# Sixty-four transposes of a two-layer hybrid decoder trunk: TensorE with an identity, or VectorE in 32 x 32 squares

## The chip, the core and the metric

The kernel runs on one core of a Trainium2 chip. The metric is the device time of one launch in microseconds (us), lower is better. A core has TensorE (PE in the profile; PEld is its weight load), VectorE (DVE), ScalarE (ACT), GpSimd (POOL) and the queue engine SyncE (SP). SBUF is the memory that all engines work in, PSUM the one that TensorE writes to; both have 128 partitions.

## The reference

A trunk of two layers works on x, 256 positions by 2048 numbers, in fp32. Each layer normalises x and multiplies it by `w_in` (2048 x 7700). Four parallel groups of 4 heads, 512 columns each, use the result:

```python
h = rms_norm(x, norm_g)
p = split_columns(jnp.einsum("bsd,de->bse", h, w_in))
fox = from_heads(forgetting_attention(q, k, v, log_f)) * silu(p["fox_g"])   # softmax attention with a forget bias
diff = rms_norm(differential_attention(...), diff_norm_g) * silu(p["diff_g"])
moba = from_heads(moba_attention(...)) * silu(p["moba_g"])                  # 256 positions: one block, causal attention
gla = from_heads(rms_norm(gla_chunked(...), gla_norm_g)) * silu(p["gla_g"]) # gated linear attention
mixed = jnp.concatenate([fox, diff, moba, gla], axis=-1)
x = x + jnp.einsum("bse,ed->bsd", mixed, w_out)
```

After the second layer a last `rms_norm` follows.

## The kernel before

**The large products.** `w_in` and `w_out` come from memory in steps of 512 KB (two or four blocks of 128 rows of the weights, "k-tiles"). ScalarE rounds each step to a high part `hi`, VectorE subtracts it for the low part `lo` (`parts_of`, `hi_of`, `lo_of`), and TensorE forms three products, high by high, low by high and high by low. The activations are kept with their 2048 numbers on the partitions, transposed, and split in the same way: `hTp` (the normalised x, high and low) for `w_in`, `mTh` and `mTl` (the four groups' results) for `w_out`. There are four buffers for the raw weights and four for each part. In the main loop (line 1335) step i + 3 is prepared (`prepare`), then step i is multiplied (`multiply`), then the small work gets a turn (`tick`).

**The small work.** All that lies between the large products is written as generators, one per group and purpose, in a list `tasks`. `tick` lets each of them go on to its next `yield`, so that their instructions fall between two steps of the large products. `Costed` adds up an assumed time for each VectorE and ScalarE instruction, and `give_time` grants as much as TensorE's matmuls are assumed to take; a tick stops while more is used than granted. So the program order on every engine is fixed when the kernel is built. Tiles are handed out by `Slots`: eight of 128 x 1024 in SBUF (`s4`, named `four`), six of 128 x 512 (`s2`, `two`), two of 128 x 1024 in PSUM (`side`). A generator that finds no free slot yields until there is one.

**The three places.** Everything that must stand the other way round is transposed by TensorE, with an identity, 128 x 128 at a time, into a `side` tile (`transpose`, line 286, matmul at L288 in the profile; all other matmuls of this part are at L284):

- `make_hT` (line 422) prepares x for the second layer, in four chunks of 512 columns, each as soon as the output projection of the first layer has added its chunk to `xs`: `turn_x` makes 8 transposes, `split_x` makes high and low parts from PSUM.
- `finish_rows` (line 506) normalises and gates the output rows of the differential and of the linear attention (`mixed`) and transposes them, 8 transposes per group and layer.
- `transposed_p` (line 729) transposes the softmax probabilities: `p0` (queries 0 to 127, keys 0 to 127) and `p1` (queries 128 to 255, all 256 keys), 8 and 4 transposes, with a copy by ScalarE to `pta` and one by VectorE to `ptb`. All three softmax attentions call it; the forgetting and the block attention through `attend_columns` (line 760), which then forms the output with v:

```python
matmul(o[:, h], vn[:, 0, h * P:(h + 1) * P], pta[:, h], True, False)
matmul(o[:, h, P:], vn[:, 1, h * P:(h + 1) * P], ptb[:, h], False, True)
```

The order of the layer's blocks is: linear attention, forgetting attention, differential attention, block attention, then four chunks of the output projection, whose k-tiles begin with the linear attention's and end with the block attention's. In the first layer x comes transposed from memory, so `make_hT` runs for the second layer alone.

Of the kernel before, what the change touches and what calls it, by code (L numbers as in the profile page):

```python
# [21 lines left out]
P = 128  # L22
SEQ = 256
# [3 lines left out]
H = 4  # L27
# [190 lines left out]
def hybrid_trunk(  # L218
# [18 lines left out]
    v_ = Costed(nc.vector, 0.06, 1.05e-3)  # L237
# [12 lines left out]
    s4 = Slots(wk, "four", T4)  # L250
    s2 = Slots(wk, "two", T2)
    s8 = Slots(wk, "eight", 1)
    sgs = Slots(wk, "gate", 2)
    side = Slots(sd, "side", 2)

    def take_side():
        return (yield from side.take([P, 1024]))
# [24 lines left out]
    def matmul(out, lhsT, rhs, start, stop, tiles=1):  # L282
        left["pe"] += int(np.prod(rhs.shape[1:])) * (4 if lhsT.dtype == F32 else 1) / 2400.0 / tiles
        t_.matmul(out, lhsT, rhs, start=start, stop=stop)  # L284

    def transpose(out, src):
        left["pe"] += 0.109
        t_.transpose(out, src, ident)  # L288


    ct = cp.tile([P, KEPT], F32, name="ct")
    ngt = cp.tile([P, DEPTH, KT], F32, name="ngt")
    xs = big.tile([P, 2, D], F32, name="xs")
# [86 lines left out]
    def before_pow(ss, n, inv):  # L380
        t = sm.tile([P, 8], F32, name="pw")
        v_.tensor_scalar(t[:, :n], ss, inv, EPS, op0=OP.mult, op1=OP.add)
        return t[:, :n]

    def power(dst, t, n):
        g_.tensor_tensor(dst, t, halfpow[:, :n], op=OP.pow)  # L386

    def hi_of(hi, src, scale=1.0):
        a_.activation(hi, src, AF.Copy, scale=scale)

    def lo_of(lo, src, hi):
        v_.tensor_sub(lo, src, hi.bitcast(F32))
# [7 lines left out]
    def turn_x(ps, chunk):  # L400
        for k in range(4):
            for m in range(2):
                kt = chunk * 4 + k
                transpose(ps[:, k * 256 + m * P:k * 256 + (m + 1) * P], xs[:, m, kt * P:(kt + 1) * P])

    def split_x(ps, l, chunk):

        cols = [(chunk * 4 + k, ps[:, k * 256:(k + 1) * 256]) for k in range(4)]
        for kt, src in cols:
            hi_of(hT[0][:, kt], src, ngt[:, l, kt:kt + 1])  # L410
        for kt, src in cols:
            v_.scalar_tensor_tensor(hT[1][:, kt], src, ngt[:, l, kt:kt + 1], hT[0][:, kt].bitcast(F32),
                                    op0=OP.mult, op1=OP.subtract)
        side.put(ps)
        ready.add(("h", l, chunk))

    def squares(l, chunk, parts):
        for m in range(2):
            square_sum(parts, m, slice(chunk * 512, chunk * 512 + 512), chunk)
        ready.add(("sq", l, chunk))  # L420

    def make_hT(l, chunk, parts):
        if chunk < 3:
            yield
        ps = yield from take_side()
        turn_x(ps, chunk)
        yield
        split_x(ps, l, chunk)
        yield
        squares(l, chunk, parts)  # L430

# [49 lines left out]
    def transposes(nat):  # L481

        ps = yield from take_side()
        for h in range(H):
            for m in range(2):
                transpose(ps[:, h * 256 + m * P:h * 256 + (m + 1) * P], nat[:, m, h * P:(h + 1) * P])
        return ps

    def split_group(l, gi, src, release):
        kts = slice(gi * 4, gi * 4 + 4)  # L490
        hi_of(mT[0][:, kts], src)
        yield
        lo_of(mT[1][:, kts], src, mT[0][:, kts])
        release()
        ready.add(("m", l, gi))
# [10 lines left out]
    def finish_rows(l, gi, o, ops, scale, sg):  # L506

        sq = yield from s4.take([P, 2, H, HD])
        a_.activation(sq, o, AF.Square)
        yield  # L510
        ss = sm.tile([P, 2, H], F32, name="ssh")
        v_.tensor_reduce(ss, sq, axis=AX.X, op=OP.add)
        s4.put(sq)
        if scale is not None:
            v_.tensor_mul(ss, ss, scale)
            v_.tensor_mul(ss, ss, scale)
        t = before_pow(ss.rearrange("p m h -> p (m h)"), 8, 1.0 / HD)
        rs = sm.tile([P, 2, H], F32, name="rsh")
        power(rs.rearrange("p m h -> p (m h)"), t, 8)
        yield  # L520
        yield
        if scale is not None:
            v_.tensor_mul(rs, rs, scale)
        mixed = yield from gated_rows(l, gi, o, rs, sg)
        side.put(ops)
        sgs.put(sg)
        yield
        ps = yield from transposes(mixed)
        s4.put(mixed)
        yield  # L530
        yield from split_group(l, gi, ps.rearrange("p (h t) -> p h t", h=H), lambda: side.put(ps))
# [194 lines left out]
        side.put(ps)  # L726
        return p

    def transposed_p(p0, p1, pool0=s2, slot0=None):
        ta = yield from take_side()  # L730
        for h in range(H):
            transpose(ta[:, h * 256:h * 256 + P], p0[:, h])
            transpose(ta[:, h * 256 + P:(h + 1) * 256], p1[:, h, 0])
        pool0.put(p0 if slot0 is None else slot0)
        yield
        pta = yield from s4.take([P, H, 2, P])
        a_.activation(pta.rearrange("p h m q -> p (h m q)"), ta, AF.Copy)
        side.put(ta)
        tb = yield from take_side()
        for h in range(H):  # L740
            transpose(tb[:, h * P:(h + 1) * P], p1[:, h, 1])
        s4.put(p1)
        yield
        ptb = yield from s2.take([P, H, P])
        v_.tensor_copy(ptb.rearrange("p h q -> p (h q)"), tb[:, :512])
        side.put(tb)
        yield
        return pta, ptb

    def normalised(p0, p1, su):  # L750
        rs = sm.tile([P, 2, H], F32, name="rs")
        v_.reciprocal(rs, su)
        v_.tensor_mul(p0, p0, rs[:, 0, :, None].to_broadcast([P, H, P]))
        yield
        pv = p1.rearrange("p h j s -> p h (j s)")
        v_.tensor_mul(pv, pv, rs[:, 1, :, None].to_broadcast([P, H, SEQ]))
        yield
        return (yield from transposed_p(p0, p1))

    def attend_columns(l, gi, name, qT, kT, forget=None):  # L760

        su = sm.tile([P, 2, H], F32, name="su")
        p0 = yield from softmax_part(0, qT, kT, slice(0, P), HD ** -0.5, su, forget)
        p1 = yield from softmax_part(1, qT, kT, slice(0, P), HD ** -0.5, su, forget)
        s4.put(qT, kT)
        if forget is not None:
            forget.release()
        yield
        pta, ptb = yield from normalised(p0, p1, su)
        yield from until((name + "_v", l))  # L770
        yield from until((name + "_g", l))
        yield
        vn, sgT = env[name + "_v", l], env[name + "_g", l]
        ops = yield from take_side()
        o = ops.rearrange("p (h t) -> p h t", h=H)
        for h in range(H):
            matmul(o[:, h], vn[:, 0, h * P:(h + 1) * P], pta[:, h], True, False)
            matmul(o[:, h, P:], vn[:, 1, h * P:(h + 1) * P], ptb[:, h], False, True)
        s4.put(pta, vn)
        s2.put(ptb)  # L780
        yield
        mixed = yield from s4.take([P, H, SEQ])
        v_.tensor_mul(mixed, o, sgT)
        side.put(ops)
        sgs.put(sgT)
        yield
        yield from split_group(l, gi, mixed, lambda: s4.put(mixed))
# [20 lines left out]
    class Forget:  # L808
# [16 lines left out]
        def release(self):  # L825
            s4.put(*self.fg)
            s2.put(*self.f1)
# [135 lines left out]
    def diff(l):  # L963
# [4 lines left out]
        scale = 64 ** -0.5  # L968
        su = [sm.tile([P, 2, H], F32, name="su") for _ in range(2)]
# [13 lines left out]
        ps = yield from take_side()  # L983
# [9 lines left out]
        p0 = yield from s4.take([P, 2, H, P])  # L993
        for i in range(2):
            for h in range(H):
                c = i * H + h
# [20 lines left out]
        p1 = []  # L1017
# [12 lines left out]
        c = sm.tile([P, 2, H], F32, name="nr")  # L1030
        v_.tensor_mul(c, rs[1], su[0])
        v_.tensor_scalar(c, c, lam[:, l:l + 1], -1.0, op0=OP.mult, op1=OP.mult)
        for m, a, b in ((0, p0[:, 0], p0[:, 1]), (1, p1[0], p1[1])):
            for h in range(H):
                v_.scalar_tensor_tensor(a[:, h], b[:, h], c[:, m, h:h + 1], a[:, h], op0=OP.mult, op1=OP.add)
            yield
        s4.put(p1[1])
        pta, ptb = yield from transposed_p(p0[:, 0], p1[0], s4, p0)
        yield from until(("diff_v", l))
        yield  # L1040
        vn = env["diff_v", l]
        ops = yield from take_side()
        o = ops.rearrange("p (m h d) -> p m h d", m=2, h=H)
        for h in range(H):
            matmul(o[:, 0, h], pta[:, h, 0], vn[:, 0, h * P:(h + 1) * P], True, True)
        for h in range(H):
            matmul(o[:, 1, h], pta[:, h, 1], vn[:, 0, h * P:(h + 1) * P], True, False)
            matmul(o[:, 1, h], ptb[:, h], vn[:, 1, h * P:(h + 1) * P], False, True)
        s4.put(pta, vn)
        s2.put(ptb)  # L1050
        yield
        yield from until(("diff_g", l))
        yield from finish_rows(l, 1, o, ops, rs[0], env["diff_g", l])
# [86 lines left out]
    for z in _BLOCKS:  # L1140
        if z["half"] != 1:
            l, f = next(dones)
# [5 lines left out]
    for z in _steps():  # L1148
        b = blocks[z["block"]]
# [185 lines left out]
    for i, s in enumerate(plan):  # L1335
# [3 lines left out]
        if i in X_AT:  # L1339
            c = slice(X_AT.index(i) * 512, X_AT.index(i) * 512 + 512)  # L1340
# [11 lines left out]
    b = plan[-1]["block"]  # L1352
# [29 lines left out]
```

## Time and profile before

| | |
|---|---|
| device time, median of 3 runs | 948.75 us (948.12 to 948.85) |
| profiled execution, its own time | 950.85 us |
| its span, first to last instruction | 949.1 us |
| instructions | 13841 |
| TensorE matmuls, busy | 5430, 938.4 us |
| VectorE, busy | 836 instructions, 613.7 us |
| ScalarE, busy | 653 instructions, 482.5 us |
| granted TensorE clock, mean of the core | 0.996 |

Busy times of the engines overlap; their sum is no time. The ends of matmuls are modelled, so a busy TensorE isn't one at its peak. An fp32 matmul leaves two records. Nearly all VectorE and ScalarE instructions have one line, L188, that of the helper which books their costs; they are told apart by their tiles.

### The profile page before, as it was taken

How to read it: one execution, taken by the hardware profiler on the slowest of the kernel's cores; microseconds unless marked ns; L12 is line 12 of the kernel's file. 1: busy time of each engine (PE TensorE's matmuls, PEld its weight loads, DVE VectorE, ACT ScalarE, POOL GpSimd, SP SyncE). 2: the span in 40 equal slices, each digit the busy share in tenths (PEclk: the TensorE clock that was granted, in tenths of full speed). 3: DMA queues.
4: the chain of work that ended last, by engine and by line, in shares of the span. 5: the costliest groups of instructions: out<-in, count | busy, mean ns of one | idle time of the engine just before them, and what ended most of it. 6: DMA issues, size and time to landing. Idle time of an engine off the chain costs nothing.

```text
span 949.1 us, 13841 instructions
## 1 busy us (share of the span) xinstructions
PE 938.4 (99%) x5430; PEld 823.0 (87%) x5430; DVE 613.7 (65%) x836; ACT 482.5 (51%) x653; POOL 68.4 (7%) x45
## 2 busy tenths in 40 slices
PE   9999999999999999999999999999999999999996
PEld 7889899888888888888898899898888898888886
DVE  7566785657756786455556667656675759755563
ACT  7575534454474446445446544446446644564451
POOL 0010201001110210000000102100011002100000
PEclk9999999999999999999999999999999999999998
DMA  8766555455656465566655544554555645754552
GB/s 298 225 186 214 185 185 173 140 172 179 198 170 178 147 206 176 159 193 182 189 172 175 165 149 156 168 176 156 167 189 177 198 152 178 238 179 160 195 178 89
DMA packets 49076, 170.19 MB, mean 179 GB/s; under 512 B 5969, under 2 KB 6513, under 8 KB 49010
## 3 DMA queue, kind: packets, MB, share of 16 engines
q1 hardware_dynamic: 46592, 165.24, 54.8%
q10 hardware_dynamic: 1778, 1.97, 0.9%
q0 software_dynamic: 640, 2.10, 0.9%
q8 instruction: 42, 0.69, 0.3%
q14 instruction: 24, 0.20, 0.1%
HBM read 167.19 MB, written 2.10 MB: 178 GB/s over the span
## 4 chain that ended last, share of the span: by engine, by line
PE 95%; DMA 2%; DVE 1%; issue 1%; ACT 0%; SPq 0%; POOLq 0%; POOL 0%; DVEq 0%; ACTq 0%
PE mm L284 86%; PE side L284 8%; PE side L288 2%; DMA raw<-in_weights 1%; DMA four<-in_xt 1%; DVE lo L188 0%; ACT hi L188 0%; DVE xs L188 0%; ACT hTp L188 0%; DVE four L188 0%; SPq L1159 0%; POOLq L1378 0%; POOL rf L386 0%; ACT two L188 0%; SPq L1172 0%
## 5 line engine op out<-in xcount | busy, mean ns | idle before, releaser
L188 DVE TENSOR_TENSOR lo<-raw,hi 128x1024 fp32r<-128x1024 f32 (+3 forms) x301 | 380.0, 1269 | 288.1 <-ACT hi L188 287.7
L188 ACT ACTIVATE hi<-raw 128x1024 fp32r<-128x1024 f32 (+3 forms) x301 | 318.4, 1060 | 406.5 <-PE mm L284 373.2
L284 PE MATMUL mm<-hTp,hi 128*128 128x512 f32 x1120 | 273.1, 392 | 0.0
L284 PEld LDWEIGHTS mm<-hTp,hi 128*128 128x128 f32 x1120 | 204.3, 188 | 39.4 <-issue 0.3
L284 PE MATMUL mm<-hi,hTp 128*128 128x512 f32 (+2 forms) x1024 | 196.6, 339 | 0.3 <-ACT hi L188 0.3
L284 PEld LDWEIGHTS mm<-hi,hTp 128*128 128x128 f32 x1024 | 159.8, 188 | 22.0 <-ACT hi L188 0.8
L284 PE MATMUL mm<-hTp,lo 128*128 128x256 f32 x1120 | 150.0, 284 | 0.0
L284 PEld LDWEIGHTS mm<-hTp,lo 128*128 128x128 f32 x1120 | 144.8, 191 | 5.9
L284 PE MATMUL mm<-lo,hTp 128*128 128x512 f32 (+2 forms) x512 | 104.9, 336 | 0.1
L284 PEld LDWEIGHTS mm<-lo,hTp 128*128 128x128 f32 x512 | 81.3, 188 | 10.4 <-DVE lo L188 0.3
L284 PE MATMUL mm<-hi,mTh 128*128 128x512 f32 (+1 forms) x256 | 65.1, 378 | 0.0
L284 PE MATMUL mm<-hi,mTl 128*128 128x512 f32 (+1 forms) x256 | 64.4, 376 | 0.0
L284 PE MATMUL mm<-lo,mTh 128*128 128x512 f32 (+1 forms) x256 | 64.4, 376 | 0.0
L284 PEld LDWEIGHTS mm<-hi,mTl 128*128 128x128 f32 x256 | 46.2, 188 | 8.8
L284 PEld LDWEIGHTS mm<-lo,mTh 128*128 128x128 f32 x256 | 46.2, 188 | 8.7
L284 PEld LDWEIGHTS mm<-hi,mTh 128*128 128x128 f32 x256 | 45.7, 188 | 8.3
L284 PE MATMUL side<-four,four 128*128 128x128 f32 (+2 forms) x288 | 38.0, 288 | 0.0
L920 POOL TENSOR_TENSOR four<-four,two 128x1024 f32<-128x1024 f32 x8 | 20.9, 2607 | 222.4 <-DVE four L188 222.4
L188 ACT ACT_TABLE_LOAD x27 | 34.6, 1283 | 2.0 <-DVE an L188 1.5
L284 PEld LDWEIGHTS side<-four,four 128*128 128x128 f32 (+1 forms) x288 | 31.5, 190 | 2.6 <-issue 1.4
L188 DVE TENSOR_TENSOR both<-mm,both 128x512 f32<-128x512 f32 x35 | 23.9, 684 | 0.0
L386 POOL TENSOR_TENSOR rsh<-pw,halfpow 128x8 f32<-128x8 f32 x4 | 10.4, 2590 | 152.1 <-DVE pw L188 152.1
(159 smaller groups left out, 620.8 us busy)
## 6 DMA issues: line engine op xcount, KB each, us to landing
raw<-in_weights SPq DMA_DIRECT2D x272, 512.0 KB, 3.8
raw<-in_weights SPq DMA_DIRECT2D x16, 516.0 KB, 3.7
raw<-in_weights SPq DMA_DIRECT2D x15, 528.0 KB, 4.6
xs<-in_x SPq DMA_DIRECT2D x4, 512.0 KB, 4.5
four<-in_xt SPq DMA_DIRECT2D x3, 512.0 KB, 7.5
out<-xs SPq DMA_DIRECT2D x6, 256.0 KB, 3.1
two<-in_const POOLq DMA_DIRECT2D x4, 256.0 KB, 3.4
two<-in_final_norm_g POOLq DMA_DIRECT2D x4, 256.0 KB, 5.7
```

Source lines behind the costliest of these rows:

```text
L188: return f(*args, **kw)
L284: t_.matmul(out, lhsT, rhs, start=start, stop=stop)
L288: t_.transpose(out, src, ident)
L386: g_.tensor_tensor(dst, t, halfpow[:, :n], op=OP.pow)
L920: g_.tensor_mul(sw, sw, over(f[:, 1], H))
```

## The change

A new helper `turned` transposes a 128 x 128 block, or several side by side, on VectorE: for each of the 4 x 4 squares of 32 partitions by 32 columns one `transpose` instruction, which takes that square of all blocks of the tile together. It yields after each four. It is used for chunks 0 to 2 of x, for the gated rows of the linear attention (`scale is None`) and for the probabilities of the forgetting attention. The fourth chunk of x, the differential attention and the probabilities of the other attentions stay on TensorE. The result lies in SBUF (`s4`, `s2`) and not in PSUM, and is split from there. Since the forgetting attention's probabilities now come in three tiles, `attend_columns` multiplies by three tiles of 128 columns, for the block attention too.

```diff
+    def turned(dst, src):
+        for j in range(4):
+            for i in range(4):
+                a, b = slice(32 * i, 32 * i + 32), slice(32 * j, 32 * j + 32)
+                v_.us += 0.14
+                v_.transpose(dst[(b,) + (slice(None),) * (len(dst.shape) - 2) + (a,)],
+                             src[(a,) + (slice(None),) * (len(src.shape) - 2) + (b,)])
+            yield
...
     def make_hT(l, chunk, parts):
         if chunk < 3:
             yield
-        ps = yield from take_side()
-        turn_x(ps, chunk)
-        yield
-        split_x(ps, l, chunk)
+        if chunk < 3:
+            t = yield from s4.take([P, 4, SEQ])
+            rows = xs[:, :, chunk * 512:chunk * 512 + 512].rearrange("p m (k c) -> p m k c", k=4)
+            yield from turned(t.rearrange("p k (m t) -> p m k t", m=2), rows)
+            split_x(t.rearrange("p k t -> p (k t)"), l, chunk)
+            s4.put(t)
+        else:
+            ps = yield from take_side()
+            turn_x(ps, chunk)
+            yield
+            split_x(ps, l, chunk)
+            side.put(ps)
...
+        if scale is None:
+            t = yield from s4.take([P, H, SEQ])
+            yield from turned(t.rearrange("p h (m t) -> p m h t", m=2), mixed.rearrange("p m (h d) -> p m h d", h=H))
+            s4.put(mixed)
+            yield from split_group(l, gi, t, lambda: s4.put(t))
+            return
         ps = yield from transposes(mixed)
...
-    def transposed_p(p0, p1, pool0=s2, slot0=None):
+    def transposed_p(p0, p1, by_rows, pool0=s2, slot0=None):
+        if by_rows:
+            pt0 = yield from s2.take([P, H, P])
+            yield from turned(pt0, p0)
+            pool0.put(p0 if slot0 is None else slot0)
+            pt1 = yield from s4.take([P, H, 2, P])
+            yield from turned(pt1, p1)
+            s4.put(p1)
+            return [pt0, pt1[:, :, 0], pt1[:, :, 1]], lambda: (s2.put(pt0), s4.put(pt1))
...
-        pta, ptb = yield from normalised(p0, p1, su)
+        pt, release = yield from normalised(p0, p1, su, name == "fox")
...
         for h in range(H):
-            matmul(o[:, h], vn[:, 0, h * P:(h + 1) * P], pta[:, h], True, False)
-            matmul(o[:, h, P:], vn[:, 1, h * P:(h + 1) * P], ptb[:, h], False, True)
+            v0, v1 = (vn[:, j, h * P:(h + 1) * P] for j in range(2))
+            matmul(o[:, h, :P], v0, pt[0][:, h], True, True)
+            matmul(o[:, h, P:], v0, pt[1][:, h], True, False)
+            matmul(o[:, h, P:], v1, pt[2][:, h], False, True)
```

## Rows read from the trace of the kernel before

**Rows 1.** The page's busy time of each engine: us, share of the span, instructions.

```profile
PE 938.4 (99%) x5430; PEld 823.0 (87%) x5430; DVE 613.7 (65%) x836; ACT 482.5 (51%) x653; POOL 68.4 (7%) x45
```

**Rows 2.** The page's chain of work that ended last, as shares of the span by engine and by line.

```profile
PE 95%; DMA 2%; DVE 1%; issue 1%; ACT 0%; SPq 0%; POOLq 0%; POOL 0%; DVEq 0%; ACTq 0%
PE mm L284 86%; PE side L284 8%; PE side L288 2%; DMA raw<-in_weights 1%; DMA four<-in_xt 1%; DVE lo L188 0%; ACT hi L188 0%; DVE xs L188 0%; ACT hTp L188 0%; DVE four L188 0%; SPq L1159 0%; POOLq L1378 0%; POOL rf L386 0%; ACT two L188 0%; SPq L1172 0%
```

**Rows 3.** The same chain in order of time, from the first layer's output projection to the second layer's start: start, us, what.

```profile
413.77 0.87 PE side L288 x8
414.64 21.79 PE mm L284 x96
436.43 0.87 PE side L288 x8
437.30 21.81 PE mm L284 x96
459.11 0.87 PE side L288 x8
...
479.24 0.87 PE side L288 x8
480.11 14.33 PE mm L284 x104
```

**Rows 4.** The same view, first layer, the linear attention (161) and the forgetting attention (188 to 192).

```profile
161.43 0.87 PE side L288 x8
...
188.05 0.87 PE side L288 x8
188.92 2.79 PE mm L284 x16
191.71 0.44 PE side L288 x4
```

**Rows 5.** The longest waits: who waited for whom, us in total, times, longest.

```profile
ACT hi L188 <- PE mm L284: 373.2, 224, 6.0
DVE lo L188 <- ACT hi L188: 287.7, 180, 5.9
```

**Rows 6.** Groups of instructions by line and shape: busy us, mean ns of one, and the idle time before them. All transposes, and the weight load of the small fp32 matmuls.

```profile
L288 PE MATMUL side<-ct,four 128*128 128x128 f32 x88 | 13.5, 272 | 0.0
L288 PE MATMUL side<-ct,xs 128*128 128x128 f32 x32 | 4.1, 272 | 0.0
L288 PE MATMUL side<-ct,two 128*128 128x128 f32 x16 | 3.7, 272 | 0.0
L288 PE MATMUL side<-ct,an 128*16 128x128 f32 x4 | 0.8, 272 | 0.0
L284 PEld LDWEIGHTS side<-four,four 128*128 128x128 f32 x192 | 25.9, 191 | 1.2
```

**Rows 7.** Matmuls in order of time, those next to each other of one form merged: start, us from the first start to the last end, count of records. A part of the softmax scores (168.94), and the forgetting attention's output (203.16 on, one head is two lines).

```profile
168.94 1.05 PE L284 MATMUL side<-four,four 128*128 128x128 f32 x8
...
203.16 0.59 PE L284 MATMUL side<-four,four 128*128 128x256 f32 x2
203.59 0.38 PE L284 MATMUL side<-two,four 128*128 128x128 f32 x2
203.81 0.60 PE L284 MATMUL side<-four,four 128*128 128x256 f32 x2
```

**Rows 8.** Groups by line and shape, as in rows 6, of ScalarE and VectorE.

```profile
L188 ACT ACTIVATE hi<-raw 128x1024 fp32r<-128x1024 f32 x268 | 283.8, 1062 | 361.0 <-PE mm L284 335.0 <-issue 7.1 <-DMA raw<-in_weights 4.5
L188 DVE STREAM_SHUFFLE four<-both 128x512 f32<-128x512 f32 x16 | 11.8, 738 | 0.0
L188 DVE COPY two<-side 128x512 f32<-128x512 f32 x6 | 4.1, 684 | 0.0
L188 DVE TENSOR_TENSOR four<-four 128x256 f32<-128x256 f32 x2 | 0.8, 424 | 0.1
```

**Rows 9.** VectorE in order of time in the linear attention, merged as in rows 7: products that go by turns to partitions 0 to 63 and 64 to 127, and products over all partitions.

```profile
84.53 2.38 DVE L188 TENSOR_TENSOR tq<-eight,four 64x128 f32<-64x128 f32 x8
...
91.03 1.50 DVE L188 TENSOR_TENSOR eight<-eight,four 128x128 f32<-128x128 f32 x7
```

**Rows 10.** VectorE in order of time in the output projection of the first layer: the low parts of the weights, the residual sums (`xs`) and the split of x; in brackets idle time before, and what ended it.

```profile
408.55 1.23 DVE L188 TENSOR_TENSOR lo<-raw,hi 128x1024 fp32r<-128x1024 f32 x1 [1.45 <-ACT hi L188]
409.70 1.28 DVE L188 TENSOR_TENSOR xs<-mm,xs 128x512 f32<-128x512 f32 x2
411.27 1.23 DVE L188 TENSOR_TENSOR lo<-raw,hi 128x1024 fp32r<-128x1024 f32 x1 [0.30 <-ACT hi L188]
...
416.29 1.66 DVE L188 SCALAR_TENSOR_TENSOR hTp<-side,ngt,hTp 128x256 fp32r<-128x256 f32 x4 [1.07 <-ACT hTp L188]
...
455.04 1.28 DVE L188 TENSOR_TENSOR xs<-mm,xs 128x512 f32<-128x512 f32 x2
```

**Rows 11.** Busy us of each engine in stretches of 10 us (stretch, length, then PE, PEld, DVE, ACT and POOL with their counts), the granted TensorE clock as a share of full speed, the DMA share and GB/s.

```profile
30.00:40.00 10.00, 8.96 (x55) 8.41 (x56) 4.94 (x8) 3.56 (x4) 1.54 (x1) 0.83 0.66 203
...
160.00:170.00 10.00, 10.00 (x73) 9.37 (x73) 5.74 (x7) 6.34 (x14) 0.00 (x0) 1.00 0.58 202
170.00:180.00 10.00, 10.00 (x60) 8.86 (x60) 4.55 (x5) 4.03 (x11) 0.00 (x0) 1.00 0.39 109
...
190.00:200.00 10.00, 10.00 (x58) 8.66 (x56) 5.31 (x6) 6.36 (x7) 0.00 (x0) 1.00 0.62 186
200.00:210.00 10.00, 10.00 (x64) 9.04 (x63) 6.75 (x9) 4.35 (x5) 0.00 (x0) 1.00 0.52 163
210.00:220.00 10.00, 10.00 (x58) 8.79 (x57) 5.35 (x6) 4.73 (x5) 0.00 (x0) 1.00 0.51 159
```

More of the change, by code (lines that the diff above doesn't have):

```diff
@@ L413, in split_x @@
                                     op0=OP.mult, op1=OP.subtract)
-        side.put(ps)
         ready.add(("h", l, chunk))
@@ L747, in transposed_p, with normalised @@
         yield
-        return pta, ptb
-    def normalised(p0, p1, su):
+        return [pta[:, :, 0], pta[:, :, 1], ptb], lambda: (s4.put(pta), s2.put(ptb))
+    def normalised(p0, p1, su, by_rows):
         rs = sm.tile([P, 2, H], F32, name="rs")
@@ L757, in normalised @@
         yield
-        return (yield from transposed_p(p0, p1))
+        return (yield from transposed_p(p0, p1, by_rows))
     def attend_columns(l, gi, name, qT, kT, forget=None):
@@ L776, in attend_columns @@
         for h in range(H):
-            matmul(o[:, h], vn[:, 0, h * P:(h + 1) * P], pta[:, h], True, False)
-            matmul(o[:, h, P:], vn[:, 1, h * P:(h + 1) * P], ptb[:, h], False, True)
-        s4.put(pta, vn)
-        s2.put(ptb)
+            v0, v1 = (vn[:, j, h * P:(h + 1) * P] for j in range(2))
+            matmul(o[:, h, :P], v0, pt[0][:, h], True, True)
+            matmul(o[:, h, P:], v0, pt[1][:, h], True, False)
+            matmul(o[:, h, P:], v1, pt[2][:, h], False, True)
+        release()
+        s4.put(vn)
         yield
@@ L1037, in diff @@
         s4.put(p1[1])
-        pta, ptb = yield from transposed_p(p0[:, 0], p1[0], s4, p0)
+        pt, release = yield from transposed_p(p0[:, 0], p1[0], False, s4, p0)
         yield from until(("diff_v", l))
@@ L1044, in diff @@
         for h in range(H):
-            matmul(o[:, 0, h], pta[:, h, 0], vn[:, 0, h * P:(h + 1) * P], True, True)
+            matmul(o[:, 0, h], pt[0][:, h], vn[:, 0, h * P:(h + 1) * P], True, True)
         for h in range(H):
[L1047 to L1050, printed above, removed]
+            matmul(o[:, 1, h], pt[1][:, h], vn[:, 0, h * P:(h + 1) * P], True, False)
+            matmul(o[:, 1, h], pt[2][:, h], vn[:, 1, h * P:(h + 1) * P], False, True)
+        release()
+        s4.put(vn)
         yield
```

## Prediction, made before the change was run

> **What bounds the kernel now.** I read the page's busy table first, then the chain that ended last, then that chain piece by piece. The busy table gives TensorE 99% of the span, VectorE 65%, ScalarE 51% [rows 1]; what is to be seen is that only one engine is full. A full bar alone doesn't prove a bound, so the chain comes next: 95% of it is PE, and the line of the transposes, L288, has 2% of the span in it [rows 2]. The third view says what that share is made of. Between the layers the chain is an unbroken run of matmuls, and each group of eight transposes is a piece of 0.87 us in it, with 96 matmuls in 21.8 us before and after [rows 3]. The groups of the linear attention and of the forgetting attention stand in the chain in the same way: 0.87 us for eight, 0.44 us for four [rows 4]. So a transpose costs its 0.109 us in full, and nobody waits for it while TensorE would otherwise rest. The other engines run behind: ScalarE's split of the weights waited 373 us in all for TensorE to give a buffer back, and VectorE's 288 us for ScalarE [rows 5]. In this state TensorE's time is the kernel's time, and VectorE's work is free as long as it is not late.
>
> **What is removed.** The 140 transposes of the profile [rows 6] are four groups of eight of x (32), the small `an` ones (4), and those of the gated rows and the probabilities. The change takes three groups of eight of x (only the second layer makes them), eight in each layer's linear attention, and eight and four in each layer's forgetting attention: 24 + 16 + 24 = 64, and 76 stay. On TensorE that is 3 x 0.87 + 2 x 0.87 + 2 x (0.87 + 0.44) = 6.97 us [rows 3, 4]. All of it is on the path. ScalarE loses the copy of `pta`, VectorE that of `ptb`, once per layer; neither engine is on the path, so I book nothing for them.
>
> A transpose's own row says 272 ns [rows 6], but eight of them take 0.87 us and not 2.2, because they are pipelined. The Trainium skill (TensorE: Matmul & The Clock Gate, Part 4: PE-mode transpose) gives about 275 ns for a transpose in one kernel's context. The rows of this case give the same duration, and a price in the stream of 0.109 us. By the Trainium skill's figure as a price the saving would be 64 x 0.275 = 17.6 us.
>
> **What is added on TensorE.** In `attend_columns`, which the forgetting and the block attention share, the 256-column product with the first half of v becomes two of 128 columns: one more fp32 matmul for each of 4 heads, 2 attentions and 2 layers, so 16. Each leaves two records, so 32 more weight loads. Today a head takes 0.65 us from start to start (203.16 to 203.81), four records, two of 256 and two of 128 columns; 128-column records, each with its own weights, follow each other every 0.11 us (eight in 1.05 us, less the last one's 0.27, over seven) [rows 7]. Six of them make 0.66 us, so the added cost is 0.0. The other bound is a load that nothing hides: 191 ns by its row [rows 6], 32 x 0.19 = 6.1 us. I take zero, since the rows of the very size run back to back.
>
> **What is added on VectorE.** `turned` issues 16 instructions for a tile of 128 x 1024, each over 32 partitions, since each handles one of 4 x 4 squares of the partitions and columns. That makes 48 (x) + 32 (linear attention) + 32 (p1) of 32 x 256, and 32 (p0) of 32 x 128. The trace has no such instruction. The nearest rows: a 128x256 sum from tile to tile takes 424 ns, the shuffle of 128x512, the operation nearest in kind, 738 ns [rows 8]. From start to start they can overlap a little: seven 128x128 products took 1.50 us, 0.20 each. But eight 64x128 products that go by turns to the upper and the lower partitions took 2.38 us, 0.30 each: nothing overlaps [rows 9]. The transposes change their source partitions from one to the next, so I take the second case: 0.30 us for 128 elements as they stand there, and for 256 the 424 ns and a little for the gap, 0.44. Bounds: 0.34 us (0.44 less the 0.10 of overlap) and 0.74 us (a shuffle of twice the size).
> The sum is 112 x 0.44 + 32 x 0.30 = 58.9 us, less two `ptb` copies of 0.68 [rows 8]: VectorE goes from 614 to some 671 us, 71% of the span. On the path it is nothing, if each stage has room.
>
> - x. A chunk has eight weight steps of 2.72 us. VectorE spends eight times 1.15 us on `lo`, 1.28 on the residual sums and 1.66 on the split of x, together 12.1 of 21.8 us [rows 10]. The 16 transposes need 7.0 of the 9.7 us left. They are issued four to a step: 1.15 + 1.76 = 2.91 us in a step of 2.72, 0.2 late each, 0.8 after four. What may be late: a step is prepared three steps ahead, 8.2 us; less 1.06 us for `hi` and 1.23 for `lo` [rows 8, 10], 5.9 us are to spare. The three chunks are used only when the next layer begins, at 480.1 us [rows 3]. The third chunk's sums stand at 455; six steps later, at about 472, it is split. The fourth chunk, for which there is no such time, stays on TensorE.
> - Linear attention. VectorE is busy 5.74 us of 160 to 170, and 4.55 of 170 to 180 [rows 11]; 7.0 us go into 9.7 idle ones. Its result is wanted only at the output projection.
> - Forgetting attention. 16 x 0.30 + 16 x 0.44 = 11.8 us, from 188 us on. 190 to 220 leaves 4.7 + 3.3 + 4.7 = 12.6 us [rows 11]. This is the tightest place: VectorE is full for 25 us, and the eight yields move the attention's output from 203 to about 214 us. Behind it nothing waits: its rows are wanted at the output projection too, and the output is issued at least one step after the last square, so TensorE should not meet it early.
>
> `Costed` books 0.47 us for such an instruction, 1.88 us a step, beside 1.135 for `lo`, against 2.56 of credit; that stretches the tasks a little and issues nothing that VectorE can't hold. No DMA is added or moved.
>
> **The sum.** 6.97 + 0 + 0: the profiled execution's 950.85 us, of which 949.1 are span, would become 943.9. The median of the runs is 2.1 us below that execution, so 948.75 - 7.0 = 941.8.
>
> **Rivals.**
> 1. *VectorE's backlog gives part back.* In the tight stretch of each layer `lo` or a transposed tile comes later than its reserve, and TensorE stands 1 to 4 us in all. For it: the 0.8 us of room in the forgetting attention's stage. Against: the 5.9 us of reserve. 943 to 946.8.
> 2. *The added weight loads show.* 32 x 0.19 = 6.1 us; 947.9, no change. Against: the 0.11 us spacing [rows 7].
> 3. *VectorE becomes the bound; slower.* One mechanism: the price of a square. Room for x is 9.7 us for 16, 0.60 us each; with a price t the three chunks pile up 48 x (t - 0.60), and beyond 5.9 us TensorE waits. At the upper bound of 0.74 that is 0.8 us. The gain of 7.0 us is gone at t = 0.87; at 1.0 us TensorE waits 13 us and the time is 955, more if the clock falls with it, as it did to 0.83 where TensorE was busy only 8.96 of 10 us [rows 11]. Against: no row with so few elements comes near 0.87 us. The Trainium skill (VectorE: DVE Perf Modes, Rules for kernel authors) speaks for this side: it sends 128x128 transposes to TensorE where PSUM will do as a destination. By that rule the change is the wrong way round, as it trades 0.87 us of one engine for 7.0 of the other; the trace says that the 0.87 are the scarce ones.
> 4. *The transposes cost more than their spacing.* At 272 ns each 64 are worth 17.4 us: 931.3. Against: the pieces of 0.87 us.
>
> **Numbers.** The forecast, 941.8, own range 941.2 to 943: 0.66. Rival 1: 0.15. Rival 2, and other ways to within 0.2% (946.9 to 950.6, about what a measurement of this kernel can tell from no change): 0.07. Rival 3: 0.08. More gain than forecast, rival 4 among it: 0.04. So faster 0.85, same 0.07, slower 0.08. The range from 941.0 to 946.5 takes in the forecast and nearly all of rival 1.
>
> **What would show it.** L288 with 76 transposes and 1% of the chain; between 405 and 500 us no piece of L288 but the last; each 32x256 square near 0.44 us from start to start; VectorE near 71%; TensorE with 5430 - 64 + 32 = 5398 matmuls, still 99% busy; a head's output at 0.66 us; the forgetting attention's output some 10 us later. I am wrong if TensorE shows idle time released by VectorE in the three stages, if a square takes over 0.7 us, or if a head's output takes 1 us.

## Result, and the profile of the changed kernel

The changed kernel takes 941.64 us (median of 6 runs, 941.29 to 941.96), the kernel before 948.70 in the same set (948.12 to 948.85). The ratio is 0.9926, 95% interval 0.9914 to 0.9939: 7.06 us faster, where 6.97 were forecast.

The busy time of each engine and the chain that ended last, from the page of the kernel after, answer to [rows 1] and [rows 2]:

```profile
PE 929.9 (99%) x5398; PEld 816.1 (87%) x5398; DVE 669.9 (71%) x978; ACT 479.5 (51%) x651; POOL 68.3 (7%) x45
PE 95%; DVE 2%; issue 1%; DMA 1%; ACT 0%; SPq 0%; POOLq 0%; POOL 0%; DVEq 0%; ACTq 0%
```

TensorE lost 32 records (64 transposes less, 32 records more) and 8.5 us of busy time, VectorE gained 56 us and is 71% busy. TensorE is still 99% busy and 95% of the chain: the same engine sets the end, with less to do.

The chain in order of time between the layers, as in [rows 3]: start, us, what.

```profile
404.88 67.06 PE mm L284 x307
471.94 0.88 PE side L288 x8
472.82 14.34 PE mm L284 x104
```

Three of the four pieces of L288 are gone, and the matmuls around them have closed up into one piece of 67 us. Only the fourth chunk's transposes are left. The whole list of TensorE's waits for other engines (us in total, times, longest) has two entries, both in the start-up:

```profile
PE side L338 <- DVE four L333: 1.3, 1, 1.3
PE side L284 <- DVE four L188: 0.7, 1, 0.7
```

The profiled spans differ by 9.4 us (949.1 and 939.7), 2.3 more than the runs do. That excess arose before the change begins to act. Both traces have the same four matmuls of the first layer's linear attention; first the kernel before, then the kernel after (chain in order of time):

```profile
57.14 1.06 PE side L284 x4
```

```profile
54.85 1.06 PE side L284 x4
```

In the kernel before, the profiled start-up had the dip of the granted clock in its stretch from 30 to 40 us [rows 11], 0.83, a mean between the levels of 1.2 and 2.4 GHz; in the kernel after, the same stretch has 1.00:

```profile
30.00:40.00 10.00, 9.67 (x66) 9.05 (x67) 5.51 (x8) 4.02 (x4) 1.54 (x1) 1.00 0.79 231
```

From the four matmuls to the end the two spans differ by 7.1 us, like the runs.

### The profile page after: what moved, and what is told of

It reads as the page before. It is cut to its first block, busy times and chain, and to the rows that moved or that the text cites. A ratio compares the mean times of both kernels' runs of the same rounds, so it can differ in the third digit from the quotient of the medians.

```text
span 939.7 us, 13910 instructions
## 1 busy us (share of the span) xinstructions
PE 929.9 (99%) x5398; PEld 816.1 (87%) x5398; DVE 669.9 (71%) x978; ACT 479.5 (51%) x651; POOL 68.3 (7%) x45
## 4 chain that ended last, share of the span: by engine, by line
PE 95%; DVE 2%; issue 1%; DMA 1%; ACT 0%; SPq 0%; POOLq 0%; POOL 0%; DVEq 0%; ACTq 0%
PE mm L284 86%; PE side L284 8%; PE side L288 1%; DVE lo L188 1%; DMA raw<-in_weights 1%; DVE four L188 0%; DVE hTp L188 0%; ACT hTp L188 0%; DVE xs L188 0%; ACT four L188 0%; ACT hi L188 0%; SPq L1193 0%; POOLq L1412 0%; POOL rf L397 0%; ACT two L188 0%
## 5 line engine op out<-in xcount | busy, mean ns | idle before, releaser
L284 PE MATMUL side<-four,four 128*128 128x128 f32 (+1 forms) x320 | 38.3, 277 | 0.0
L284 PEld LDWEIGHTS side<-four,four 128*128 128x128 f32 (+1 forms) x320 | 35.0, 190 | 2.4 <-issue 1.4
L188 DVE STREAM_TRANSPOSE four<-four 32x256 f32<-32x256 f32 x64 | 27.9, 436 | 1.0
```

Source lines behind the costliest of these rows:

```text
L188: return f(*args, **kw)
```

## Experiments

Each was timed beside the kernel before; the ratio is to that, with its 95% interval. Gains and losses against the kernel after compare medians of different sets, between which the kernel before moved by 0.3 us (948.70 to 948.98). First the parts one by one.

**Only x.** The kernel before with `turned`, `split_x` and `make_hT` as in the change, `finish_rows`, `transposed_p` and `attend_columns` as they were.

```diff
+        if chunk < 3:
+            t = yield from s4.take([P, 4, SEQ])
+            yield from turned(t.rearrange("p k (m t) -> p m k t", m=2), rows)
...
```

> Only the three chunks of x are transposed on VectorE; the attentions are as in the kernel before. Theory (a transpose costs TensorE 0.109 us of the stream, and VectorE's squares are hidden): 24 x 0.109 = 2.6 us less, 946.1. Rival (the gain came from freed PSUM slots and a changed order of the tasks, not from the transposes themselves): no fixed relation to the 24, and the gains of the three parts need not add up to 7.0. Rival (VectorE's backlog gives part back here): less than 2 us.

946.04 us against 948.90, ratio 0.9967 (0.9955 to 0.9980): 2.9 us less.

**Only the linear attention's rows.** The kernel before with the change's `finish_rows`.

```diff
+        if scale is None:
+            t = yield from s4.take([P, H, SEQ])
+            yield from turned(t.rearrange("p h (m t) -> p m h t", m=2), mixed.rearrange("p m (h d) -> p m h d", h=H))
...
```

> Only the linear attention's gated rows are transposed on VectorE. Theory: 16 x 0.109 = 1.7 us less, 947.0. Rival (order of tasks and PSUM slots): no relation to the 16. Rival (backlog): VectorE is full from 150 to 172 us, so the low part of a weight step comes late and less than 1 us is gained.

947.23 us, ratio 0.9984 (0.9976 to 0.9993): 1.7 us less.

**Only the forgetting attention's probabilities**, with the output in three pieces.

```diff
-        pta, ptb = yield from normalised(p0, p1, su)
+        pt, release = yield from normalised(p0, p1, su, name == "fox")
...
```

> Only the forgetting attention's probabilities are transposed on VectorE, with the output product in three pieces of 128 columns. Theory: 24 x 0.109 = 2.6 us less, nothing added, 946.1. Rival (the 32 added weight loads show, 0.19 us each): 2.6 less and 6.1 more, 952. Rival (backlog in the tightest place): 947 to 948.7.

946.29 us, ratio 0.9978 (0.9967 to 0.9988): 2.6 us less.

**Only the output in three pieces**, all transposes on TensorE.

```diff
-            matmul(o[:, h], vn[:, 0, h * P:(h + 1) * P], pta[:, h], True, False)
+            matmul(o[:, h, :P], v0, pt[0][:, h], True, True)
+            matmul(o[:, h, P:], v0, pt[1][:, h], True, False)
...
```

> All transposes stay on TensorE; only the output product of the forgetting and the block attention is cut in three pieces of 128 columns. Theory: 0.0, 948.7. Rival (the added weight loads show): up to 6.1 us more, 954.8.

948.90 us, ratio 0.9999 (0.9990 to 1.0008): nothing. The parts' gains of 2.9, 1.7 and 2.6 stand in the proportion of their 24, 16 and 24 transposes and add up to 7.1 us, as much as all together. The intervals are about 1 us to either side. The profiled executions agree more closely: counted from the same four matmuls of the first layer to the end, the three parts are 2.8, 2.0 and 2.5 us shorter than the kernel before, and the output in three pieces alone is 0.2 us longer. A gain through freed PSUM slots or another order of the tasks would have no reason to. The added weight loads don't show.

**How near the edge: x's squares issued twice.** The second issue writes the same values again.

```diff
+                for _ in range(again):
+                    nc.vector.transpose(d, s)
```

> The kernel after, each square of the three chunks of x issued twice (the second writes the same again; it is not booked in the task budget, so the order of the rest is the same): 21 us more on VectorE. Forecast's formula (room 0.60 us a square, 5.9 us of reserve): 48 x (0.88 - 0.60) - 5.9 = 7.5 us of waiting, 949. Rival (the reserve is larger than 5.9, or the room is found again between the chunks): under 943. Rival (no reserve, the 21 us all show): 962.

963.08 us, ratio 1.0140 (1.0125 to 1.0155): 21.4 us above the kernel after, as much as VectorE got to do. The forecast's formula said 7.5. TensorE's two longest waits (the second is that of the fourth chunk's transposes):

```profile
PE mm L284 <- DVE lo L188: 7.4, 6, 2.0
PE side L288 <- issue: 5.5, 1, 5.5
```

Busy time in stretches (columns as in [rows 11]):

```profile
440.00:450.00 10.00, 7.94 (x34) 5.90 (x32) 9.52 (x19) 1.06 (x1) 0.00 (x0) 1.00 0.32 105
450.00:460.00 10.00, 7.24 (x24) 5.56 (x25) 8.85 (x16) 5.50 (x11) 0.00 (x0) 0.83 0.39 114
...
480.00:490.00 10.00, 4.75 (x25) 4.30 (x23) 8.94 (x15) 6.80 (x12) 0.00 (x0) 0.67 0.54 158
```

VectorE (third) is full and TensorE (first) is not: here VectorE is the bound, and where TensorE rested the granted clock fell to 0.83 and 0.67 as means of ten microseconds, so part of it ran at the lower level, 1.2 GHz. The waits make 12.9 of the 21.4 us; the other 8.5 are put down to this clock, which was not measured apart. The formula had only the wait for the low parts, 7.5 us. That 7.4 were measured is no support for it, since its room in each chunk was too large, as the next kernel shows.

**Half of them twice** (`again if i < 2 else 0`).

> As the kernel with the squares of x issued twice, but only every second square is repeated: 24 squares more, 11 us more on VectorE, 0.67 us per square in effect. Forecast's formula: 48 x (0.67 - 0.60) = 3.4 us of pile-up, under the 5.9 of reserve, so nothing shows: 941.6. Theory formed since (VectorE's lateness is not forgiven: ScalarE stands in its queue for the split of x, the next raw weights are fetched late, and the last chunk's sums come late): a chunk needs 12.1 + 24 x 0.455 = 23.0 of 21.8 us, 1.2 us late each, and what is late at the end shows in full: 944 to 947.

951.81 us, ratio 1.0030 (1.0019 to 1.0041): 10.2 us above the kernel after, for 11 us of squares. So the gain was gone long before the price of 0.87 us a square that the forecast named. TensorE in order of time, with the only waits (in brackets) that it had between 400 and 480 us:

```profile
468.48 1.20 PE L284 MATMUL mm<-lo,mTh 128*128 128x512 f32 x4 [0.29 <-DVE lo L188]
...
472.54 1.24 PE L284 MATMUL mm<-lo,hTp 128*128 128x264 f32 x8 [0.93 <-DVE lo L188]
...
479.27 2.31 PE L288 MATMUL side<-ct,xs 128*128 128x128 f32 x8 [5.49 <-issue]
```

The weights come late by little, 1.2 us: their reserve holds nearly as computed. What has none is the fourth chunk's transposes on TensorE: they want the sums `xs`, and these stand in VectorE's queue behind all that is late. The profile names no releaser for these 5.5 us ("issue"); that it was the sums is read from the times, as the first sum starts at 478.49 and the transposes at 479.27. Behind the wait the eight transposes took 2.31 us, where they took 1.04 in the kernel after, and the sixteen matmuls that follow 3.87 and not 2.19; the granted clock is 0.74 and 0.75 in the stretches from 470 to 490 us. That makes most of the 3.5 us that the waits leave of the 10.2. VectorE's sums of the chunks in this kernel, and then in the kernel after:

```profile
429.84 1.28 DVE L188 TENSOR_TENSOR xs<-mm,xs 128x512 f32<-128x512 f32 x2
...
454.11 1.28 DVE L188 TENSOR_TENSOR xs<-mm,xs 128x512 f32<-128x512 f32 x2
...
478.49 1.28 DVE L188 TENSOR_TENSOR xs<-mm,xs 128x512 f32<-128x512 f32 x2
```

```profile
426.92 1.28 DVE L188 TENSOR_TENSOR xs<-mm,xs 128x512 f32<-128x512 f32 x2
...
448.68 1.28 DVE L188 TENSOR_TENSOR xs<-mm,xs 128x512 f32<-128x512 f32 x2
...
470.50 1.28 DVE L188 TENSOR_TENSOR xs<-mm,xs 128x512 f32<-128x512 f32 x2
```

2.9, 5.4 and 8.0 us late: some 2.6 us more with each chunk, for 8 x 0.455 = 3.6 us of squares. So a chunk in the kernel after leaves about 1 us of usable room, where the forecast had 9.7 less 7.0 = 2.7. Two things make the difference. A low part and four squares take 3.07 us from start to start, where the forecast had 2.91, so 0.7 us a chunk; in the kernel after:

```profile
454.41 1.78 DVE L188 STREAM_TRANSPOSE four<-xs 32x256 f32<-32x256 f32 x4
...
457.48 1.79 DVE L188 STREAM_TRANSPOSE four<-xs 32x256 f32<-32x256 f32 x4
```

The other 0.9 us are time in which VectorE waits for ScalarE, as the views of both engines in the kernel with half of the squares twice show (ScalarE first):

```profile
422.69 1.71 ACT L188 ACTIVATE hTp<-four,ngt 128x256 fp32r<-128x256 f32 x4 [5.09 <-DVE four L188]
424.31 1.04 ACT L188 ACTIVATE hi<-raw 128x1024 fp32r<-128x1024 f32 x1
...
430.45 1.06 ACT L188 ACTIVATE hi<-raw 128x1024 fp32r<-128x1024 f32 x1 [1.02 <-DMA raw<-in_weights]
```

```profile
427.56 2.36 DVE L188 TENSOR_TENSOR lo<-raw,hi 128x1024 fp32r<-128x1024 f32 x2 [0.93 <-ACT hi L188]
```

ScalarE stands 5.1 us at the split of x until the last square is done (1.3 in the kernel after), the next weights' `hi` behind it; and since a late `lo` gives its raw buffer back late, the next raw weights are late too (1.02 us of waiting for the DMA).

**The forgetting attention's squares issued twice.**

```diff
-            yield from turned(pt0, p0)
+            yield from turned(pt0, p0, 1)
...
-            yield from turned(pt1, p1)
+            yield from turned(pt1, p1, 1)
```

> The kernel after, each square of the forgetting attention's probabilities issued twice, not booked: 11.8 us more on VectorE in each layer, at the place that the forecast called the tightest. Forecast's sizes (0.8 us of room, 5.9 of reserve): 11.8 - 0.8 - 5.9 = 5 us of waiting in each layer, 952. Rival (the tasks were stretched over 30 us and not 25, so there was more room): 941.6 to 944.

962.98 us, ratio 1.0141 (1.0126 to 1.0157): 21.3 us above the kernel after, for 23.6 us of squares. TensorE's longest waits, and two stretches of the first layer (columns as in [rows 11]):

```profile
PE mm L284 <- DVE lo L188: 13.5, 6, 3.7
```

```profile
220.00:230.00 10.00, 6.83 (x29) 5.82 (x30) 9.71 (x15) 2.60 (x3) 2.55 (x1) 0.83 0.31 102
230.00:240.00 10.00, 7.21 (x33) 6.04 (x33) 9.63 (x17) 2.28 (x3) 0.00 (x0) 0.83 0.44 145
```

Here it is the weights' low parts that come late. The forecast's sizes gave 5 us a layer after room and reserve; the waits are 6.9 us in the first layer and 6.6 in the second. In all 10.7 a layer were lost: to the 13.5 us of waiting come, as in the stretches shown, matmuls at a lower granted clock. How much of the remaining 7.8 us these make was not traced.

**The fourth chunk of x on VectorE too.**

```diff
-        if chunk < 3:
+        if chunk < 4:
             t = yield from s4.take([P, 4, SEQ])
```

> The kernel after, with the fourth chunk of x on VectorE too. Theory (a square is free only while its tile is not yet wanted): TensorE saves another 0.9 us, but the second layer's first block wants the fourth chunk after three steps, 8 us. VectorE needs 16 x 0.44 = 7.0 us for it, three low parts of 1.15 and the split of about 3 us lie between, 13.5 us in all, so TensorE stands about 4 to 6 us: 945 to 947. Rival (off the path it is free everywhere): 940.8.

954.01 us, ratio 1.0052 (1.0039 to 1.0065): 12.4 us above the kernel after, more than twice the expected loss. TensorE at the second layer's start, with its two waits:

```profile
475.03 2.11 PE L284 MATMUL mm<-hi,hTp 128*128 128x264 f32 x16
...
483.74 3.89 PE L284 MATMUL mm<-hi,hTp 128*128 128x264 f32 x16 [5.64 <-ACT hTp L188]
...
503.91 3.18 PE L284 MATMUL mm<-hTp,hi 128*128 128x512 f32 x8 [3.71 <-ACT gate L188]
```

The first is the expected wait, 5.6 us. The second was not: `make_hT` makes the squared sums for the row norm after its split, so the norm came later and the first block's results could not be taken from PSUM. The rest is the clock: after the first wait the sixteen matmuls took 3.89 us, where sixteen of the kind took 2.11 before it; the granted clock is 0.66 in the stretch from 480 to 490 us.

**The differential attention's probabilities on VectorE too.**

```diff
-        pt, release = yield from transposed_p(p0[:, 0], p1[0], False, s4, p0)
+        pt, release = yield from transposed_p(p0[:, 0], p1[0], True, s4, p0)
```

> The kernel after, with the differential attention's probabilities on VectorE too: 24 more transposes off TensorE. Theory: their output waits for the block's own order only, VectorE is busy 3.27 of 10 us right behind (300 to 310 us), so 24 x 0.109 = 2.6 us less, 939.0. Rival (that output's rows come later and push into the full stretch of 310 to 340 us, so VectorE's backlog reaches TensorE): 940 to 944.

939.76 us, ratio 0.9901 (0.9887 to 0.9914): the fastest kernel of the study. Its median is 1.9 us below that of the kernel after, but the two were timed in different sets and its five runs lie between 938.98 and 941.40. The profiled spans are the better sign: 937.2 against 939.7, with the same start-up (54.95 us to the matmuls shown above), so 2.6 us as expected. VectorE is full from 290 to 320 us (columns as in [rows 11]), and TensorE doesn't notice:

```profile
290.00:300.00 10.00, 10.00 (x58) 8.75 (x57) 9.66 (x20) 4.00 (x5) 0.00 (x0) 1.00 0.51 159
300.00:310.00 10.00, 10.00 (x61) 8.90 (x60) 9.71 (x19) 3.94 (x5) 0.10 (x1) 1.00 0.61 170
310.00:320.00 10.00, 10.00 (x61) 8.90 (x60) 9.79 (x13) 4.45 (x5) 2.58 (x1) 1.00 0.52 166
```

**The differential attention's gated rows too**, alone, and together with its probabilities (then with the edit above).

```diff
-        if scale is None:
+        if True:
             t = yield from s4.take([P, H, SEQ])
```

> The kernel after, with the differential attention's gated rows on VectorE and its probabilities left on TensorE: 16 more transposes, 1.7 us if hidden: 939.9. Its rows come at 320 us, where VectorE is busy 9.96 of 10 us and 8.90 in the next 10. Theory (room at the place): part of it is lost, 940 to 943. Rival (hidden): 939.9.

> The kernel after, with the differential attention's probabilities and its gated rows on VectorE: 24 + 16 more transposes off TensorE, 36 in effect 4.4 us if all is hidden: 937.3. VectorE is then busy 9.7 of 10 us from 290 to 320 and about 9.9 from 340 to 350, where the rows' 7.0 us would fall. Theory (room counts at the place, not over the span): TensorE waits there, 938 to 943, no better than with the probabilities alone (939.8). Rival (room over 340 to 380 is enough): 937.3 to 938.

(The "36" in the second expectation is a slip for 24 + 16 = 40.) The rows alone gave 947.17 us, ratio 0.9985 (0.9976 to 0.9993); both gave 945.65, 0.9965 (0.9951 to 0.9978). The rows cost 5.5 us against the kernel after, and 5.9 against the kernel with the probabilities alone. The wait had been sought at the place of the squares; half of it in the first kernel and all of it in the second lies later. TensorE's waits of the kernel with the rows alone, then with both:

```profile
PE mm L284 <- ACT mTh L188: 2.4, 2, 1.2
PE mm L284 <- DVE lo L188: 2.3, 2, 1.1
```

```profile
PE mm L284 <- ACT mTh L188: 4.8, 2, 2.4
```

`mTh` is the split of the block attention's result, the last that the output projection wants. In the chain its output begins at 393.9 us with both, at 386.2 with the probabilities alone. With both, the granted clock was 0.95, 0.88 and 0.83 in the stretches beside the wait (390 to 400, 400 to 410 and 860 to 870 us), which adds to the loss; with the rows alone it was 1.00 in all three. How the losses divide was not traced. That the block attention is late because its task stands behind the differential attention's in the list and in the budget of the ticks is argued from `tick`, not shown.

**The block attention's probabilities on VectorE.**

```diff
-        pt, release = yield from normalised(p0, p1, su, name == "fox")
+        pt, release = yield from normalised(p0, p1, su, True)
```

> The kernel after, with the block attention's probabilities on VectorE: 24 more transposes, 2.6 us. Their output is wanted soon: the output projection has begun by then, and its k-tiles 8 to 11 need it some 10 us later. The squares take 11.8 us of VectorE, and the eight yields some 25 us. Theory (a square is free only while its tile is not yet wanted): TensorE stands 10 us or more in each layer, 955 or more. Rival (VectorE is only half busy there, so it is hidden): 939.0.

949.76 us, ratio 1.0013 (1.0004 to 1.0021): 8.1 us worse than the kernel after, well short of the 955 or more that were expected. TensorE waits for the squares and for the split behind them, as expected, but 8.5 us in both layers together, where 10 or more in each were expected:

```profile
PE mm L284 <- ACT mTh L188: 4.8, 2, 2.4
PE side L284 <- DVE four L188: 3.7, 3, 1.3
```

## Why the prediction was right, and where its steps were off

**Removed.** 6.97 us forecast, 7.06 measured; by parts 2.61, 1.74 and 2.62 forecast, 2.9, 1.7 and 2.6 measured. The step that carried it was to take a transpose's price from its piece in the chain, 0.109 us, and not its duration of 272 ns, by which rival 4 had 17.4 us. The Trainium skill's figure for the duration (TensorE: Matmul & The Clock Gate, Part 4: PE-mode transpose), about 275 ns, agrees with the rows, and is no price here.

**Added on TensorE.** 0.0 forecast, 0.0 measured. One head of the output in the kernel after (229.07 to 229.74), as in [rows 7]:

```profile
229.07 0.39 PE L284 MATMUL side<-two,four 128*128 128x128 f32 x2
229.29 0.61 PE L284 MATMUL side<-four,four 128*128 128x128 f32 x4
229.74 0.39 PE L284 MATMUL side<-two,four 128*128 128x128 f32 x2
```

0.67 us, 0.66 forecast, 0.65 before.

**Added on VectorE.** The squares in the kernel after, by line and shape:

```profile
L188 DVE STREAM_TRANSPOSE four<-four 32x256 f32<-32x256 f32 x64 | 27.9, 436 | 1.0
L188 DVE STREAM_TRANSPOSE four<-xs 32x256 f32<-32x256 f32 x48 | 20.9, 436 | 0.8
L188 DVE STREAM_TRANSPOSE two<-two 32x128 f32<-32x128 f32 x32 | 9.7, 302 | 0.5
```

436 and 302 ns, with 10 to 20 ns between two of them; forecast were 0.44 and 0.30 us from start to start. The alternating products of [rows 9] were the right neighbours. VectorE's total, 669.9 us, was forecast at 671.

**Hidden.** Right for all three places, as the lone parts and the two entries of TensorE's list of waits show.

**The forgetting attention's output.** Forecast some 10 us later; it came 28 us later (203.3 before, 229.2 after, in a trace whose start-up was 2.3 us shorter). This cost nothing, but the step was wrong. The lone parts split it: lines of the chain with the second part of the scores (x22) and the output, for the kernel with all transposes on TensorE, then the linear attention alone, then the forgetting attention alone:

```profile
165.94 3.35 PE side L284 x22
...
201.26 2.68 PE side L284 x24
```

```profile
175.61 3.17 PE side L284 x22
...
207.96 2.62 PE side L284 x16
```

```profile
165.88 3.36 PE side L284 x22
...
219.33 2.68 PE side L284 x24
```

The linear attention's squares alone hold the forgetting attention's scores back by 9.7 us and its output by 6.7; its own squares take 18 us more than the transposes on TensorE, not 10. Some 3 us come only with both. The forecast had counted one step for a yield and only this attention's own squares. That it waits for the others because its task stands behind theirs in the list, and because they draw on the same budget, is argued from `tick`, not shown.

**Rival 3's price.** Its mechanism is real, and what decides it was mis-sized. The forecast had the gain gone at 0.87 us a square; with 0.67 in effect the kernel is already 3 us slower than before. The room per chunk was taken as all of VectorE's idle time, 2.7 us, though only about 1 can be used, and the only reader of VectorE's work was taken to be the weights, with 5.9 us of reserve. The fourth chunk's sums, which TensorE wants almost at once, have none. So the place of x was hidden by a smaller margin than computed: that it could be hidden was reasoned from the rows, that its room sufficed was in part luck.

The Trainium skill (VectorE: DVE Perf Modes, Rules for kernel authors) sends such transposes to TensorE where PSUM will do as a destination. In this kernel that holds for the fourth chunk, the block attention and the differential attention's rows (12.4, 8 and 5.5 us lost on VectorE), and not for the other places (7.1 us gained, and some 2 more with the differential attention's probabilities).

## What to carry to other kernels

Where one engine is the chain, work taken off it is worth its spacing in that chain, times its count, and not its duration; add it up and test it part by part. Work put on a half-idle engine is free only where its own tile is wanted late *and* the next thing in that engine's queue that the full engine wants at once still comes in time: look for the reader without a reserve, here the last chunk's sums or the last group's result, before dividing idle time by a price. A free place is a place, not a share of the span: at 71% busy, squares at one more place gained 2 us and at the next lost 5.

## What the runs showed of the hardware beyond the forecast

A square issued a second time, on the same partitions as the one before, started no earlier than one that changes them: 407.90, 408.36 and 408.81 us in the kernel with x's squares twice, 0.46 and 0.45 apart, for a duration of 0.43:

```profile
407.90 0.42 DVE L188 STREAM_TRANSPOSE four<-xs 32x256 f32<-32x256 f32 x1
408.36 0.43 DVE L301 STREAM_TRANSPOSE four<-xs 32x256 f32<-32x256 f32 x1
408.81 0.43 DVE L188 STREAM_TRANSPOSE four<-xs 32x256 f32<-32x256 f32 x1
```

The second is the repeated one. So no overlap was seen either way; whether it is the transpose itself or that the second writes the same tile was not tried.
